# Small inputs in four host-laid arrays through SP's and ACT's queues, and 26 shared slots instead of 24, in a two-layer decoder trunk

## The chip, the cores and the metric

The kernel runs on one core of a Trainium2 chip. The metric is the time of one execution in microseconds on the device; lower is better. Five engines take part: TensorE (PE) for the matmuls, VectorE (DVE), ScalarE (ACT) and GpSimd (POOL) for work on vectors, and SyncE (SP), which here only issues DMAs. Each engine runs its own instructions in order, and semaphores tie the engines together. A DMA is issued by one engine and then runs on the 16 DMA engines that all of them share. PE's clock is granted by a throttle; the profile gives it as a share of full speed.

## The reference

```python
for l in range(DEPTH):                                   # 2 layers, 256 tokens, width 1024
    mix = token_mixer(x, w_in[l], ..., w_gate[l], b_gate[l], w_a[l], w_b[l], w_c[l], w_o[l], ...)
    x = layer_norm(alpha * x + mix, ln1_g[l], ln1_b[l])
    ffn = hier_moe(x, w_group[l], b_group[l], w_sub[l], b_sub[l], w1[l], w3[l], w2[l])
    x = layer_norm(alpha * x + ffn, ln2_g[l], ln2_b[l])

def hier_moe(...):
    g_prob = softmax(t @ w_group + b_group)              # 4 groups of experts, the best one is taken
    sub    = t @ w_sub + b_sub                           # 32 experts, the best two of that group
    ...
    for e in range(N_EXPERTS):                           # each a SwiGLU of width 256
        h = silu(t @ w1[e]) * (t @ w3[e])
        y = y + combine[:, e:e + 1] * (h @ w2[e])
```

The token mixer has three attention branches (latent, dilated, and sparse with a learned index) on one input projection; each branch is projected, multiplied by a gate and summed, and an output projection follows. All is float32. The inputs that the change concerns are the small ones: norm gains and biases (`q_norm_g`, `kv_norm_g`, `ln1_*`, `ln2_*`), gate biases and the router's weights and biases (`w_group`, `b_group`, `w_sub`, `b_sub`).

## The kernel before

Each of the two layers is a mixer and then an expert stage (`moe`). In the profile layer 0's mixer takes the first 290 us or so, its expert stage ends near 500; layer 1 is the same half again. The mixer's large matmuls are split in high and low parts (the lines 283 to 285), which makes them long; the expert stage goes through 32 experts in eight groups of four (`Q = 4`). For a group all four `w1` are used, then all four `w3` (both at L1697), then all four `w2` (L1777). An expert has three weights of 1 MiB: a group has 12 MiB.

All weights come through one pool of `NSLOT` shared slots, each 2048 floats (8 KB) in each of the 128 partitions, that is 1 MiB. The same slots hold other large tiles: `x`, the router's weights for the next layer (`wr`), the masks, and the gain rows (`gb`). The weights have a fixed order, the ring's queue. `Ring.pump` runs each time a slot is given back in the program and issues further weights as long as the plan (recorded in a dry run) says that slots suffice until their end (`fits`). So the ring runs ahead of the matmuls: where the program is about to work on one group, the issues of the next group or more already stand in SP's instruction stream. All weights are issued by SP, each with a wait for its slot's last reader. Eight DMA semaphores take turns for SP's transfers, and each issue waits for the transfer eight places ahead. In the last group of a layer `w3` comes in 16 transfers of 256 KB (four tiles, each with two of the eight parts of the width for all four experts), and `w2` in pieces of 512 KB and 256 KB; L195 issues whole tiles and L193 the pieces. The warm-up matmuls L291 work on no data of the result.

The small inputs are loaded by POOL. `load_small` (L398 to L417) fills `vec` row by row from seven arrays and the router's tile from two in a strided pattern, and the biases; for layer 0 at the start, for layer 1 in the expert stage of layer 0, after the third group (`e == 2 * Q`). `small_T` transposes `vec` on PE (L423) and scales the router on POOL; `small_rows` (L440) makes sums of it on PE. At L1326, in the mixer's output projection, `gpk` gets the first norm's gains in a packed form for the expert stage (L1660). At L1804, after the sixth group (`e == NE - 3 * Q`), `load_gains` (L447) takes a slot `gb` and loads the second norm's gain and bias as one row each; after the seventh group (`e == NE - 2 * Q`) `spread_gains` copies them to all partitions by eight PE passes (L458), and the last group follows.

The rules of the ring and the places of the gain row:

```python
while self.plan and not self.hold and self.queue and self.fits(self.queue[0][0]):
    self.issue()
...
if e == NE - 3 * Q:
    self.gb2 = self.load_gains(l, 2, 1)
...
if e == NE - 2 * Q:
    self.spread_gains(self.gb2)
```

Of the kernel before, what the change touches and what calls it, by code (L numbers as in the profile page):

```python
# [10 lines left out]
F32 = mybir.dt.float32  # L11
# [4 lines left out]
ALU = mybir.AluOpType  # L16
# [3 lines left out]
P = 128  # L20
L = 2
T = 256
NT = 2
D = 1024
KD = 8
# [19 lines left out]

WO = [(0, 512), (512, 256), (768, 256)]

NSLOT = 24
T1 = 5


# [61 lines left out]
CONSTS, MASKS = constants()  # L113
# [115 lines left out]
class Trunk:  # L229
# [26 lines left out]

    def tap(self, name, ap):
        if name in self.dbg:
            self.nc.gpsimd.dma_start(self.dbg[name], ap)
# [137 lines left out]

    def load_small(self, l, home, o):  # L398

        nc, a = self.nc, self.a  # L400
        v = self.v = self.t([P, P], F32, "vec", 1)
        nc.gpsimd.memset(v, 0.0)
        nc.gpsimd.dma_start(v[0:2], a["q_norm_g"][l].rearrange("(k p) -> k p", p=P))
        nc.gpsimd.dma_start(v[2:3], a["kv_norm_g"][l:l + 1])
        nc.gpsimd.dma_start(v[3:27], a["b_gate"][l].rearrange("(k p) -> k p", p=P))
        nc.gpsimd.dma_start(v[27:35], a["ln1_g"][l].rearrange("(k p) -> k p", p=P))
        nc.gpsimd.dma_start(v[35:43], a["ln1_b"][l].rearrange("(k p) -> k p", p=P))
        m = max(l - 1, 0)
        nc.gpsimd.dma_start(v[43:51], a["ln2_g"][m].rearrange("(k p) -> k p", p=P))
        nc.gpsimd.dma_start(v[51:59], a["ln2_b"][m].rearrange("(k p) -> k p", p=P))  # L410
        self.wgs = home
        self.wgb = home[:, o:o + KD * 72].rearrange("p (k f) -> p k f", k=KD)
        nc.gpsimd.dma_start(self.wgb[:, :, 36:40], a["w_group"][l].rearrange("(k p) f -> p k f", p=P))
        nc.gpsimd.dma_start(self.wgb[:, :, 40:72], a["w_sub"][l].rearrange("(k p) f -> p k f", p=P))
        self.br = self.t([1, 36], F32, "br", 1)
        nc.gpsimd.dma_start(self.br[:, 0:4], a["b_group"][l:l + 1])
        nc.gpsimd.dma_start(self.br[:, 4:36], a["b_sub"][l:l + 1])  # L417

    def small_T(self):

        nc = self.nc
# [7 lines left out]
        w = self.wgb[:, :, 36:72]  # L429
        for j in range(2):  # L430
            g = self.vec[:, 27 + 8 * j:35 + 8 * j, None].broadcast_to([P, KD, 36])
            nc.gpsimd.tensor_tensor(self.wgb[:, :, 36 * j:36 * j + 36], w, g, op=ALU.mult)
        nc.gpsimd.tensor_copy(self.wg, self.wgb[:, :, 0:36])

    def small_rows(self):

        nc = self.nc
        ps = self.bank()
        for k in range(KD):
            nc.tensor.matmul(ps[:, 0:72], self.one.broadcast_to([P, P]), self.wgb[:, k], start=k == 0, stop=False)  # L440
        nc.tensor.matmul(ps[:, 36:72], self.one[0:1].broadcast_to([1, P]), self.br, start=False, stop=True)
        self.wrow = self.t([P, 72], F32, "wrow", 1)
        nc.vector.tensor_copy(self.wrow, ps[:, 0:72])
        self.slots.free(self.wgs)

    def load_gains(self, l, which, rows=P):
        gb = self.slots.alloc([P, 2, D], F32, "gb")  # L447
        for j, n in enumerate(("g", "b")):
            self.nc.gpsimd.dma_start(gb[:rows, j], self.a[f"ln{which}_{n}"][l:l + 1].broadcast_to([rows, D]))
        return gb  # L450

    def spread_gains(self, gb):
# [846 lines left out]
    def mixer(self, l, acts):  # L1299
        nc = self.nc  # L1300
        prep, do = self.prep, self.do
        ps, nfill, n_wo = self.marks
        for a in START[l].split():
            if a in acts:
                acts[a]()
            elif a[0] == "m":
                do(int(a[1]), int(a[2]))
            else:
                self.lo_pool = a[0] == "P"
                prep(int(a[1:]))  # L1310
                self.lo_pool = False
        debt = 0.0
        for i in range(4, nfill - 4):
            need = ps[i][3]
            if need is not None and need not in self.seen:
                self.run_fg_until(need)
            for part in range(2):
                do(i, part)
                if part:
                    for j in range(1, 1 + (LA if i < LATE else LA_LATE)):  # L1320
                        prep(i + j)
                debt = self.run_fg(self.rate(i + 0.5 * part) / 2 + debt)
# [356 lines left out]
    def moe(self, l):  # L1679
        nc = self.nc  # L1680
# [8 lines left out]
        for e in range(0, NE, Q):  # L1689
# [238 lines left out]
def kernel(ctx: ExitStack, tc: tile.TileContext, a, out, dbg=None):  # L1928
# [3 lines left out]
    Trunk(tc, ctx, a, out, dbg, (dry.slots.log, dry.ring.ends)).run()  # L1932


_INS = ["x", "w_in", "q_norm_g", "w_uq", "kv_norm_g", "w_ukv", "w_gate", "b_gate", "w_a", "w_b", "w_c", "w_o",
        "ln1_g", "ln1_b", "w_group", "b_group", "w_sub", "b_sub", "w1", "w3", "w2", "ln2_g", "ln2_b"]


# [17 lines left out]
```

## Time and profile before

| | us |
|---|---|
| median of 3 runs | 1011.29 (1007.78 to 1011.47) |
| the profiled execution | 1009.72 |
| its span | 1008.0 |
| its clock granted to PE, mean | 0.953 of full speed |
| PE busy | 903.2 |
| DMA moved | 284.76 MB, 283 GB/s in the mean |

The profile is of one execution. Its page has the span in 40 slices (25.2 us each), the chain of work that ended last, the waits by line, and the DMA issues. The trace behind it gives a time line of each engine: the start of an instruction (or of a run of like ones), its length, and in brackets how long the engine had been idle and what ended that. The time line of SP shows when a DMA is issued; the table of DMAs says how long after that its data landed, as a median of the group.

### The profile page before, as it was taken

What the parts mean: (1) busy time and instruction counts of PE and PEld (TensorE: products, weight loads), DVE (VectorE), ACT (ScalarE), POOL (GpSimd) and SP (SyncE); (2) the same over time, 40 slices, a digit from 0 to 9 for tenths busy, and PEclk for the clock granted to TensorE, in tenths of its full rate; (3) what the DMA queues carried; (4) which work ended last, traced back from release to release, by engine and by line L of the source; (5) the groups of instructions that cost most, each with busy time, mean ns of one, the idle gap of its engine ahead of it and who ended that gap; (6) DMA issues with size and microseconds to landing.
All of it is one profiled execution on the core that took longest, in us unless ns stands there. A gap on an engine that the chain in (4) does not pass through costs nothing.

```text
span 1008.0 us, 18682 instructions
## 1 busy us (share of the span) xinstructions
PE 903.2 (90%) x7590; PEld 707.6 (70%) x7591; DVE 476.8 (47%) x968; ACT 419.4 (42%) x911; POOL 161.3 (16%) x274
## 2 busy tenths in 40 slices
PE   8999999999999976759879999999999998876595
PEld 7888899999985543435469888998999764443252
DVE  5848676944643100111398586777446521101014
ACT  5545655644462410122345645666344532210131
POOL 4531110012100110000156071100211000000001
PEclk9999999999999978789989999999999999877798
DMA  9933171596979999999992233516959799999995
GB/s 330 329 114 125 53 241 43 181 351 221 354 264 405 416 400 419 418 417 383 366 382 81 73 125 105 190 55 222 339 217 366 276 403 417 420 419 416 419 367 175
DMA packets 100170, 284.76 MB, mean 283 GB/s; under 512 B 6324, under 2 KB 53808, under 8 KB 78576
## 3 DMA queue, kind: packets, MB, share of 16 engines
q1 hardware_dynamic: 99088, 283.12, 74.5%
q8 instruction: 62, 1.02, 0.4%
q0 software_dynamic: 992, 0.39, 0.2%
q14 instruction: 28, 0.23, 0.1%
HBM read 282.44 MB, written 1.05 MB: 281 GB/s over the span
## 4 chain that ended last, share of the span: by engine, by line
PE 60%; DMA 22%; issue 7%; POOL 3%; DVE 3%; ACT 2%; SPq 1%; POOLq 0%; DVEq 0%; ACTq 0%
DMA w<-in_w_dram 20%; PE bank L283 13%; PE bank L284 12%; PE bank L285 12%; PE bank L1697 6%; PE bank L837 3%; PE bank L1777 2%; PE bank L891 2%; PE bank L878 2%; PE bank L1656 2%; DMA w<-in_w_in_dram 1%; PE bank L840 1%; PE bank L1763 1%; ACT xp L1438 1%; PE bank L1465 1%
## 5 line engine op out<-in xcount | busy, mean ns | idle before, releaser
L279 DVE TENSOR_TENSOR ws<-w,ws 128x1024 fp32r<-128x1024 f32 (+2 forms) x154 | 184.6, 1207 | 133.1 <-ACT ws L278 124.2
L1697 PE MATMUL bank<-w,xg 128*32 128x256 f32 x2048 | 150.0, 428 | 68.3 <-DMA w<-in_w_dram 59.1
L1697 PEld LDWEIGHTS bank<-w,xg 128*32 128x32 f32 x2048 | 71.9, 122 | 148.1 <-DMA w<-in_w_dram 70.1
L278 ACT ACTIVATE ws<-w 128x1024 fp32r<-128x1024 f32 (+2 forms) x158 | 158.9, 1023 | 35.7 <-PE bank L285 15.9
L283 PE MATMUL bank<-ws,xTh 128*128 128x408 f32 (+3 forms) x320 | 116.0, 362 | 1.2 <-ACT xTh L278 1.2
L283 PE MATMUL bank<-xTh,ws 128*128 128x256 f32 x384 | 111.2, 290 | 0.0
L285 PE MATMUL bank<-ws,xTl 128*128 128x408 f32 (+3 forms) x320 | 110.0, 344 | 1.1 <-DVE xTl L279 1.1
L284 PE MATMUL bank<-ws,xTh 128*128 128x408 f32 (+3 forms) x320 | 109.7, 343 | 0.2 <-DVE ws L279 0.2
L284 PE MATMUL bank<-xTl,ws 128*128 128x256 f32 x384 | 108.6, 283 | 0.0
L285 PE MATMUL bank<-xTh,ws 128*128 128x256 f32 x384 | 108.5, 283 | 0.0
L1727 DVE SCALAR_TENSOR_TENSOR t<-t,cw,bank 128x256 f32<-128x256 f32 x16 | 10.8, 677 | 200.5 <-PE bank L1697 200.5
L1660 ACT ACTIVATE xg<-bank,gpk 128x128 f32<-128x128 f32 x128 | 50.9, 453 | 95.3 <-PE bank L1656 92.7
L283 PEld LDWEIGHTS bank<-xTh,ws 128*128 128x128 f32 x384 | 73.5, 191 | 1.8 <-issue 1.0
L284 PEld LDWEIGHTS bank<-xTl,ws 128*128 128x128 f32 x384 | 73.6, 192 | 0.2
L285 PEld LDWEIGHTS bank<-xTh,ws 128*128 128x128 f32 x384 | 73.5, 191 | 0.0
L1722 ACT ACTIVATE t<-bank 128x256 f32<-128x256 f32 x16 | 6.2, 384 | 147.3 <-PE bank L1697 147.3
L283 PEld LDWEIGHTS bank<-ws,xTh 128*128 128x128 f32 x320 | 60.8, 190 | 8.1 <-ACT xTh L278 1.8
L853 ACT ACTIVATE p<-bank,nb 128x128 f32<-128x128 f32 (+1 forms) x92 | 37.3, 420 | 69.8 <-DVE nb L845 65.0
L285 PEld LDWEIGHTS bank<-ws,xTl 128*128 128x128 f32 x320 | 60.7, 190 | 6.2 <-DVE xTl L279 2.0
L1656 PE MATMUL bank<-xg,xp 128*128 128x128 f32 x512 | 63.0, 276 | 2.0 <-ACT xg L1660 2.0
L1656 PEld LDWEIGHTS bank<-xg,xp 128*128 128x128 f32 x512 | 60.6, 192 | 5.9 <-issue 2.5
L284 PEld LDWEIGHTS bank<-ws,xTh 128*128 128x128 f32 x320 | 60.9, 190 | 3.6 <-DVE ws L279 0.5
(361 smaller groups left out, 1587.6 us busy)
## 6 DMA issues: line engine op xcount, KB each, us to landing
w<-in_w_dram SPq DMA_DIRECT2D x168, 1024.0 KB, 19.0
w<-in_w_gate_dram SPq DMA_DIRECT2D x24, 1024.0 KB, 5.4
w<-in_w_dram SPq DMA_DIRECT2D x80, 256.0 KB, 6.9
w<-in_w_in_dram SPq DMA_DIRECT2D x18, 1024.0 KB, 9.6
w<-in_w_in_dram SPq DMA_DIRECT2D x12, 816.0 KB, 12.5
w<-in_w_o_dram SPq DMA_DIRECT2D x8, 1024.0 KB, 8.8
w<-in_w_a_dram SPq DMA_DIRECT2D x4, 1024.0 KB, 5.9
w<-in_w_c_dram SPq DMA_DIRECT2D x4, 1024.0 KB, 5.1
```

Source lines behind the costliest of these rows:

```text
L278: self.nc.scalar.activation(hi, src, AF.Copy)
L279: (self.nc.gpsimd if self.lo_pool else self.nc.vector).tensor_tensor(lo, src, hi.bitcast(F32), op=ALU.subtract)
L283: m(out, sh, mh, start=start, stop=False)
L284: m(out, sh, ml, start=False, stop=False)
L285: m(out, sl, mh, start=False, stop=stop)
L837: nc.tensor.matmul(b[:, j * w:(j + 1) * w], q[:, blk * P:(blk + 1) * P], k[:, 0:w], start=j == 0, stop=False)
L853: nc.scalar.activation(p[:, j], v[:, j], AF.Exp, bias=nb[:, j:j + 1], scale=u["scale"], accum_out=sm[:, j:j + 1])
L878: nc.tensor.transpose(ps[:, n * P:(n + 1) * P], p[:, j * P:(j + 1) * P], self.ident)
L891: nc.tensor.matmul(ps[half * 64:(half + 1) * 64, pr * P:(pr + 1) * P], u["v"](u["heads"][pr], kb), u["pt"][:, u["pt0"] + pr * nkb + kb], s ...
L1656: nc.tensor.matmul(ps[:, i * P:(i + 1) * P], self.xn[:, t, k + i], pm[:, t, j:j + Q].rearrange("p e c -> p (e c)"), start=t == 0, stop=t = ...
L1660: nc.scalar.activation(xg[:, k + i], ps[:, i * P:(i + 1) * P], AF.Identity, bias=b, scale=g)
L1697: nc.tensor.matmul(hp[i * CAP:(i + 1) * CAP, c * 256:(c + 1) * 256], xg[:, k, i * CAP:(i + 1) * CAP], w[i], start=k == 0, stop=k == KD - 1 ...
```

## The change

The host lays the small inputs out in four arrays: `vecs` (128 rows of 164 floats for each layer: the rows of `vec`, and the router's biases behind row 0), `router` (128 x 288), `gpk` (128 x 16) and `ln2` (one row of 2 x 1024). POOL issues no DMA any more. ACT loads `vecs` and `router` of layer 0 at the start; SP loads those of layer 1, `gpk` and `ln2`, at the same places of the program as before. As POOL issues nothing, its descriptor memory goes down to 64 bytes, and with the room that leaves the slots go from 24 to 26. The router's tile has the scaled and the plain weights as two blocks instead of side by side, with the views changed to fit.

```diff
-NSLOT = 24
+NSLOT = 26
...
     def load_small(self, l, home, o):
...
         nc, a = self.nc, self.a
-        v = self.v = self.t([P, P], F32, "vec", 1)
-        nc.gpsimd.memset(v, 0.0)
-        nc.gpsimd.dma_start(v[0:2], a["q_norm_g"][l].rearrange("(k p) -> k p", p=P))
...
-        nc.gpsimd.dma_start(v[51:59], a["ln2_b"][m].rearrange("(k p) -> k p", p=P))
+        eng = nc.sync if l else nc.scalar
+        small = self.t([P, P + 36], F32, "vec", 1)
+        eng.dma_start(small, a["vecs"][l])
+        self.v, self.br = small[:, 0:P], small[0:1, P:P + 36]
         self.wgs = home
-        self.wgb = home[:, o:o + KD * 72].rearrange("p (k f) -> p k f", k=KD)
-        nc.gpsimd.dma_start(self.wgb[:, :, 36:40], a["w_group"][l].rearrange("(k p) f -> p k f", p=P))
-        nc.gpsimd.dma_start(self.wgb[:, :, 40:72], a["w_sub"][l].rearrange("(k p) f -> p k f", p=P))
-        self.br = self.t([1, 36], F32, "br", 1)
-        nc.gpsimd.dma_start(self.br[:, 0:4], a["b_group"][l:l + 1])
-        nc.gpsimd.dma_start(self.br[:, 4:36], a["b_sub"][l:l + 1])
+        self.wgb = home[:, o:o + 2 * KD * 36].rearrange("p (j k f) -> p j k f", j=2, k=KD)
+        eng.dma_start(home[:, o + KD * 36:o + 2 * KD * 36], a["router"][l])
...
-    def load_gains(self, l, which, rows=P):
+    def load_gains(self, l):
         gb = self.slots.alloc([P, 2, D], F32, "gb")
-        for j, n in enumerate(("g", "b")):
-            self.nc.gpsimd.dma_start(gb[:rows, j], self.a[f"ln{which}_{n}"][l:l + 1].broadcast_to([rows, D]))
+        self.nc.sync.dma_start(gb[:1], self.a["ln2"][l:l + 1])
         return gb
...
             if i == n_wo - 12:
                 self.gpk = self.t([P, 2 * KD], F32, "gpk", 1)
-                for j, n in enumerate(("ln1_g", "ln1_b")):
-                    nc.gpsimd.dma_start(self.gpk[:, j * KD:(j + 1) * KD], self.a[n][l].rearrange("(p k) -> p k", p=P))
+                nc.sync.dma_start(self.gpk, self.a["gpk"][l])
...
             if e == NE - 3 * Q:
-                self.gb2 = self.load_gains(l, 2, 1)
+                self.gb2 = self.load_gains(l)
...
-    nc = _bacc.Bacc("TRN2", target_bir_lowering=False, num_devices=1)
+    nc = _bacc.Bacc("TRN2", target_bir_lowering=False, num_devices=1, dynamic_dma_scratch_size=64)
```

Where the change moves instructions, the built programs show it. The number behind a name is that of the tile; a `_49` in a wait only marks a semaphore.

SP before, late in layer 0's expert stage, where the weights of the last group are issued (`128x512` are pieces of `w3`, `128x2x512` of `w2`):

```order
L193 DMA w_4644<-in_w_dram 128x512 [waits DMAHW0_49,PE_49]
L193 DMA w_4644<-in_w_dram 128x512 [waits DMAHW1_49]
L193 DMA w_4644<-in_w_dram 128x512 [waits DMAHW2_49]
L193 DMA w_4644<-in_w_dram 128x512 [waits DMAHW3_49]
L193 DMA w_4649<-in_w_dram 128x2x512 [waits DMAHW4_49,PE_49]
L193 DMA w_4649<-in_w_dram 128x2x512 [waits DMAHW5_49]
L193 DMA w_4652<-in_w_dram 128x2x512 [waits DMAHW6_49,PE_49]
L193 DMA w_4652<-in_w_dram 128x2x512 [waits DMAHW7_49]
```

SP after, at the same place:

```order
L193 DMA w_4585<-in_w_dram 128x512 [waits DMAHW5_49,PE_49]
L193 DMA w_4585<-in_w_dram 128x512 [waits DMAHW6_49]
L193 DMA w_4585<-in_w_dram 128x512 [waits DMAHW7_49]
L193 DMA w_4585<-in_w_dram 128x512 [waits DMAHW0_49]
L193 DMA w_4590<-in_w_dram 128x2x512 [waits DMAHW1_49,PE_49]
L193 DMA w_4590<-in_w_dram 128x2x512 [waits DMAHW2_49]
L439 DMA gb_4593<-in_ln_dram 1x2048 [waits DMAHW3_49,PE_49]
L193 DMA w_4628<-in_w_dram 128x2x512 [waits DMAHW4_49,PE_49]
```

The gain row (`gb`, L439) now stands between the first and the second tile of the last group's `w2`, behind all `w3` of that group.

POOL before, where it loaded the gain row; the two rows ahead of it are its work on the router (`wr`) and on a gathered tile (`xg`):

```order
L433 COPY wg_4415<-wr_3907 128x288
L1647 TENSOR_TENSOR xg_3152<-xg_3152,comb_3098 128x256 [waits DVE_49] x2
L449 DMA gb_4608<-in_ln_g_dram 1x16x64 [waits DMAHW3_49,DMAHW1_49,DMAHW5_49,DMAHW0_49,DMAHW6_49,DMASW0_49,PE_49]
L449 DMA gb_4608<-in_ln_b_dram 1x16x64 [waits DMASW1_49]
L279 TENSOR_TENSOR ws_4992<-w_4699,ws_4992 128x832 [waits DMAHW3_49,DMAHW6_49,DMAHW0_49,DMAHW7_49,PE_49,Activation_49]
```

On POOL these two DMAs stood in a row of their own with no weights ahead of them; after the change POOL has none.

PE after, between the seventh group's last `w2` matmuls and the last group's first `w1` matmuls:

```order
L1766 MATMUL bank_4747<-w_4449,t_489_4712 32x512
L448 MATMUL bank_4768<-gb_4593,one 128x512 [waits DMAHW3_49,Activation_49]
L448 MATMUL bank_4771<-gb_4593,one 128x512 [waits DVE_49]
L448 MATMUL bank_4774<-gb_4593,one 128x512 [waits DVE_49]
L448 MATMUL bank_4777<-gb_4593,one 128x512 [waits DVE_49]
L1686 MATMUL bank_4784<-w_4451,xg_3438 32x256 [waits DMAHW5_49,DVE_49]
```

PE's order is the same as before; the first of the gain matmuls (L458 before, L448 after) waits for a transfer of SP's queue (`DMAHW3`), where it waited for one of POOL's (`DMASW0`).

## Rows read from the trace of the kernel before

**Rows 1.** The page: span, and PE and DMA by slices (tenths busy, 40 slices).

```profile
span 1008.0 us, 18682 instructions
...
PE   8999999999999976759879999999999998876595
...
DMA  9933171596979999999992233516959799999995
```

**Rows 2.** The page: the chain that ended last, by line, in shares of the span.

```profile
DMA w<-in_w_dram 20%; PE bank L283 13%; PE bank L284 12%; PE bank L285 12%; PE bank L1697 6%; PE bank L837 3%; PE bank L1777 2%; PE bank L891 2%; PE bank L878 2%; PE bank L1656 2%; DMA w<-in_w_in_dram 1%; PE bank L840 1%; PE bank L1763 1%; ACT xp L1438 1%; PE bank L1465 1%
```

**Rows 3.** Waits by line: us in total, times, longest us.

```profile
PE bank L1697 <- DMA w<-in_w_dram: 59.1, 15, 9.1
...
POOL wr L413 <- PE bank L1777: 20.8, 1, 20.8
...
POOL gb L449 <- PE bank L1777: 15.0, 2, 7.5
```

**Rows 4.** Time line of PE, layer 0's end: start, us, line, [idle before <- releaser].

```profile
449.04 1.06 PE L1697 MATMUL bank<-w,xg 128*32 128x256 f32 x2 [8.78 <-DMA w<-in_w_dram]
451.54 5.30 PE L1697 MATMUL bank<-w,xg 128*32 128x256 f32 x58 [1.44 <-DMA w<-in_w_dram]
457.31 3.66 PE L1697 MATMUL bank<-w,xg 128*32 128x256 f32 x64 [0.47 <-ACT t L1722]
...
470.54 3.69 PE L458 MATMUL bank<-gb,one 1*128 1x512 f32 x8
474.17 5.35 PE L1697 MATMUL bank<-w,xg 128*32 128x256 f32 x64
```

**Rows 5.** Time line of PE, layer 1's end.

```profile
947.95 1.06 PE L1697 MATMUL bank<-w,xg 128*32 128x256 f32 x2 [9.14 <-DMA w<-in_w_dram]
...
969.17 3.69 PE L458 MATMUL bank<-gb,one 1*128 1x512 f32 x8
```

**Rows 6.** Stretches: length; busy of PE, PEld, DVE, ACT, POOL; PEclk, DMA share, GB/s.

```profile
298.00:300.00 2.00, 2.00 (x44) 1.23 (x40) 0.42 (x1) 1.97 (x5) 0.00 (x0) 1.00 0.05 8
352.00:362.00 10.00, 2.43 (x16) 0.78 (x18) 0.69 (x1) 0.49 (x1) 2.89 (x4) 0.70 1.01 371
362.00:450.00 88.00, 63.98 (x623) 37.50 (x615) 10.11 (x21) 15.79 (x40) 5.33 (x9) 0.85 1.01 418
798.00:800.50 2.50, 2.50 (x49) 1.55 (x52) 0.42 (x1) 2.21 (x6) 0.00 (x0) 1.00 0.24 36
...
449.00:453.00 4.00, 2.52 (x18) 0.95 (x22) 0.00 (x0) 0.00 (x0) 0.00 (x0) 0.50 1.02 422
```

**Rows 7.** Time line of POOL, 435 to 445 us.

```profile
440.24 0.55 POOL L449 DMA_DIRECT2D gb<-in_ln_g_dram  x1 [7.50 <-PE bank L1777]
```

**Rows 8.** DMA issues: engine, count, KB each, median us from issue to landing.

```profile
w<-in_w_dram SPq DMA_DIRECT2D x168, 1024.0 KB, 19.0
...
cst<-in_consts_dram SPq DMA_DIRECT2D x1, 64.0 KB, 2.0
...
gb<-in_ln_g_dram POOLq DMA_DIRECT2D x2, 4.0 KB, 5.3
```

**Rows 9.** Time line of SP: first `w2` piece of the last group, layers 0 and 1.

```profile
478.12 0.75 SPq L193 DMA_DIRECT2D w<-in_w_dram  x1
...
976.75 0.57 SPq L193 DMA_DIRECT2D w<-in_w_dram  x1
```

**Rows 10.** DMA issues at 478.1 to 479.5 and 976.7 to 977.9 us.

```profile
w<-in_w_dram SPq DMA_DIRECT2D x2, 512.0 KB, 7.3
...
w<-in_w_dram SPq DMA_DIRECT2D x2, 512.0 KB, 7.0
```

**Rows 11.** Time line of ACT at the start: its first work on data.

```profile
5.92 1.09 ACT L278 ACTIVATE xTh<-bank 128x512 fp32r<-128x512 f32 x2 [3.66 <-PE bank L519]
```

**Rows 12.** Time line of SP at the start: the rest of the constants.

```profile
5.23 3.71 SPq L322 DMA_DIRECT2D cst<-in_consts_dram  x1
```

**Rows 13.** PE's transposes of the vectors: ns min/median/max, first and last start us.

```profile
L423 PE MATMUL bank<-cst,vec x2: 272/286/300, 32.6 to 411.6; 128*128 128x128 f32 x2
```

More of the change, by code (lines that the diff above doesn't have):

```diff
@@ L258, in tap @@
         if name in self.dbg:
-            self.nc.gpsimd.dma_start(self.dbg[name], ap)
+            self.nc.sync.dma_start(self.dbg[name], ap)
     def note(self, eng, n, psum=False):
@@ L400, in load_small @@
         nc, a = self.nc, self.a
-        v = self.v = self.t([P, P], F32, "vec", 1)
-        nc.gpsimd.memset(v, 0.0)
-        nc.gpsimd.dma_start(v[0:2], a["q_norm_g"][l].rearrange("(k p) -> k p", p=P))
[L404 to L409, printed above, removed]
-        nc.gpsimd.dma_start(v[51:59], a["ln2_b"][m].rearrange("(k p) -> k p", p=P))
-        self.wgs = home
-        self.wgb = home[:, o:o + KD * 72].rearrange("p (k f) -> p k f", k=KD)
-        nc.gpsimd.dma_start(self.wgb[:, :, 36:40], a["w_group"][l].rearrange("(k p) f -> p k f", p=P))
-        nc.gpsimd.dma_start(self.wgb[:, :, 40:72], a["w_sub"][l].rearrange("(k p) f -> p k f", p=P))
-        self.br = self.t([1, 36], F32, "br", 1)
-        nc.gpsimd.dma_start(self.br[:, 0:4], a["b_group"][l:l + 1])
-        nc.gpsimd.dma_start(self.br[:, 4:36], a["b_sub"][l:l + 1])
+        eng = nc.sync if l else nc.scalar
+        small = self.t([P, P + 36], F32, "vec", 1)
+        eng.dma_start(small, a["vecs"][l])
+        self.v, self.br = small[:, 0:P], small[0:1, P:P + 36]
+        self.wgs = home
+        self.wgb = home[:, o:o + 2 * KD * 36].rearrange("p (j k f) -> p j k f", j=2, k=KD)
+        eng.dma_start(home[:, o + KD * 36:o + 2 * KD * 36], a["router"][l])
     def small_T(self):
@@ L428, in small_T @@
         self.wg = self.t([P, KD, 36], F32, "wg", 1)
-        w = self.wgb[:, :, 36:72]
+        w = self.wgb[:, 1]
         for j in range(2):
             g = self.vec[:, 27 + 8 * j:35 + 8 * j, None].broadcast_to([P, KD, 36])
-            nc.gpsimd.tensor_tensor(self.wgb[:, :, 36 * j:36 * j + 36], w, g, op=ALU.mult)
-        nc.gpsimd.tensor_copy(self.wg, self.wgb[:, :, 0:36])
+            nc.gpsimd.tensor_tensor(self.wgb[:, j], w, g, op=ALU.mult)
+        nc.gpsimd.tensor_copy(self.wg, self.wgb[:, 0])
     def small_rows(self):
@@ L439, in small_rows @@
         for k in range(KD):
-            nc.tensor.matmul(ps[:, 0:72], self.one.broadcast_to([P, P]), self.wgb[:, k], start=k == 0, stop=False)
+            nc.tensor.matmul(ps[:, 0:72], self.one.broadcast_to([P, P]), self.wgb[:, :, k], start=k == 0, stop=False)
         nc.tensor.matmul(ps[:, 36:72], self.one[0:1].broadcast_to([1, P]), self.br, start=False, stop=True)
@@ L1932, with laid_out @@
     Trunk(tc, ctx, a, out, dbg, (dry.slots.log, dry.ring.ends)).run()
-_INS = ["x", "w_in", "q_norm_g", "w_uq", "kv_norm_g", "w_ukv", "w_gate", "b_gate", "w_a", "w_b", "w_c", "w_o",
-        "ln1_g", "ln1_b", "w_group", "b_group", "w_sub", "b_sub", "w1", "w3", "w2", "ln2_g", "ln2_b"]
+_INS = ["x", "w_in", "w_uq", "w_ukv", "w_gate", "w_a", "w_b", "w_c", "w_o", "w1", "w3", "w2"]
+def laid_out(a):
+    vecs = np.zeros((L, P, P + 36), np.float32)
+    for l in range(L):
+        m = max(l - 1, 0)
+        rows = [a["q_norm_g"][l], a["kv_norm_g"][l], a["b_gate"][l], a["ln1_g"][l], a["ln1_b"][l], a["ln2_g"][m], a["ln2_b"][m]]
+        v = np.concatenate([r.reshape(-1, P) for r in rows])
+        vecs[l, :len(v), :P] = v
+        vecs[l, 0, P:P + 4], vecs[l, 0, P + 4:] = a["b_group"][l], a["b_sub"][l]
+    router = np.concatenate([a["w_group"], a["w_sub"]], 2).reshape(L, KD, P, 36).transpose(0, 2, 1, 3).reshape(L, P, KD * 36)
+    gpk = np.concatenate([a[n].reshape(L, P, KD) for n in ("ln1_g", "ln1_b")], 2)
+    return {"vecs": vecs, "router": router, "gpk": gpk, "ln2": np.stack([a["ln2_g"], a["ln2_b"]], 1)}
 def kernel(**inputs):
@@ L1941 @@
     from concourse.bass_utils import run_bass_kernel_spmd as _run
-    nc = _bacc.Bacc("TRN2", target_bir_lowering=False, num_devices=1)
+    nc = _bacc.Bacc("TRN2", target_bir_lowering=False, num_devices=1, dynamic_dma_scratch_size=64)
     arrays, args = {}, {}
     feed = {n: inputs[n] for n in _INS}
-    feed["consts"], feed["masks"] = CONSTS, MASKS
+    feed.update(laid_out({n: np.asarray(a) for n, a in inputs.items()}), consts=CONSTS, masks=MASKS)
     for name, v in feed.items():
```

## The prediction

> **What bounds the kernel now.** I read the slices first. TensorE (PE) is busy nine tenths of the span, and its share dips at two places, late in the first half and at the end; there the DMA row stands at 9 [rows 1]. So the bound changes with the stage: PE in the mixers, the weight stream in the second part of each expert stage. The chain says the same: its largest single piece is the weights of the experts, a fifth of the span [rows 2]. The waits put a size on it: PE's expert matmuls (L1697) waited 59.1 us for weights [rows 3]. The last of these waits matter most, since what is late there ends late. In layer 0 PE stops at 449.04 for 8.78 us and at 451.54 for 1.44 us, and after that it stops for no DMA until the layer ends; the gain rows are spread at 470.54 (L458), and the first weights of the last group of four experts follow at 474.17 [rows 4]. Layer 1 repeats it about 499 us later: a wait of 9.14 us at 947.95, the gain rows at 969.17 [rows 5]. The stretch view tells since when the stream is saturated: between 298 and 300 the DMA engines are all but idle (8 GB/s), from 362 to 450 they move 418 GB/s; in layer 1 the idle stretch is 798 to 800.5 [rows 6]. Two consecutive tiles of 1 MiB let PE go on at 449.04 and 451.54: 2.50 us a tile [rows 4].
>
> **The change part by part.**
>
> **Two more slots.** The printed order shows each weight tile issued on the release that let the tile two places earlier go. At 298 to 300 the queue was empty for want of a slot; with two more slots two tiles more are then under way or done, and as the stream has no gap afterwards, each later landing comes two tiles sooner: 2 x 2.50 = 5.0 us. PE's last waits, 8.78 + 1.44 in layer 0 and 9.14 in layer 1, are longer than that, so PE passes them 5.0 us sooner in each layer, and so reaches the gain rows sooner. Bounds: 0 (if a release that is nearer to the end takes over) to 5.0; I take 5.0. By the Trainium skill ("DMA: Bandwidth & Descriptors", Specifications) memory gives a core about 358 GB/s; two tiles would then be 2.097 MB / 358 = 5.9 us. The trace does not agree: 418 GB/s over 88 us [rows 6].
>
> **POOL's router load goes.** In layer 0 POOL issues the next layer's router weights in scattered pieces at 352. From 352 to 362 the engines move 371 GB/s instead of 418 [rows 6]: 10 x (1 - 371/418) = 1.1 us are lost, and the 144 KiB that it carried are another 0.35. In their place 128 x 164 and 128 x 288 floats come in whole rows, 231 KB, 0.55 us at 418 GB/s. Net -0.9 in layer 0 (0 to -1.5), ahead of the last waits, so it counts: PE would come to the gain rows 5.9 us sooner, at 464.6, and in layer 1 5.0 sooner, at 964.2. SP must wait for the router's slot now, where POOL waited 20.8 us [rows 3]; what SP has in flight covers 19 us [rows 8], so at worst a gap of 2 us would follow. I take 0: SP comes to the slot later than POOL did, behind the tiles that the ring has run ahead with.
>
> **The gain row changes queues.** This decides. Before, POOL issues it from its own queue at 440.24 after a wait for a slot [rows 3, 7], it lands some 5.3 us later [rows 8], at about 446, and PE asks for it at 470.54: 24 us in hand. After, it stands in SP's queue, and SP is not where PE is. The order of SP shows it behind the four w1 tiles of the last group, its 16 quarter-megabyte pieces of w3 and the first two pieces of its w2, all of which the ring has queued by running ahead. Yet PE needs it *before* any of the last group's weights. A SP transfer is issued only when the one eight places ahead of it has landed (the order prints that wait on every row), and those in flight are served in turn: a 1 MiB tile lands 19 us after its issue [rows 8]. So the row's landing is that of its neighbours. The two w2 pieces ahead of it were issued before at 478.12 and 0.8 us later [rows 9] and landed 7.3 us after issue in the median [rows 10]: in the mean at 478.5 + 7.3 = 485.8; half a megabyte takes 1.3 us at 400 GB/s, so the second lands at 486.4. In layer 1: 976.75 and 0.6 later [rows 9], median 7.0 [rows 10], so 977.1 + 7.0 + 0.65 = 984.7. Taking off the stream's lead, and 0.1 for the 8 KB themselves:
> layer 0: 486.4 - 5.9 + 0.1 = 480.6, where the gain rows were spread at 470.54: +10.1 us;
> layer 1: 984.7 - 5.0 + 0.1 = 979.8, where it was 969.17: +10.6 us.
> PE would stand still for 480.6 - 464.6 = 16 us, and 15.6. All the lead is spent, and more. What comes next, the last group and the norm, is fed by weights that have landed by then or land soon after, so it follows unchanged; a queue that SP fills a few tiles ahead cannot become late by PE's pause.
> Bounds: no earlier than the issue allows. Its issue follows the second w2 piece's by 0.7 us, at 479.6 - 5.9 = 473.7 (when the eleventh w3 piece, eight places ahead, has landed); the shortest landing in the trace is 2.0 us (the 64 KB constants at the start, with an empty queue [rows 8]): 475.7, still +5.2 in layer 0 and about +5 in layer 1. The upper bound is 1 us more than I took. I take the neighbours' landing since SP's other transfers landed one after the other.
> The rows speak for separate queues: POOL's row landed in 5.3 us while SP's tiles took 19 [rows 8]. By the Trainium skill ("DMA: Bandwidth & Descriptors", Issuing engines are not separate DMA queues) the engine that issues a transfer saves only its own sequencer's time, since all run on the same 16 engines and interleave. By that rule alone the row would land as POOL's did, 5.3 us after its issue, at 479.0, and the sum would be 3 us smaller for both layers. The trace agrees with the shared engines, but shows a transfer of the other queue served well ahead of older ones.
>
> **The clock after the pause.** After the 8.78 us wait PE's granted clock is 0.50 from 449 to 453 (the lower of its two levels, 1.2 instead of 2.4 GHz) [rows 6], and 58 matmuls take 5.30 us where 64 take 3.66 at full clock [rows 4]: 5.30 - 58/64 x 3.66 = 2.0 us. The new pause is longer, and what follows it (eight gain matmuls, 3.69 us at full clock, then 64 of L1697) runs into the same: +2.0 us a layer. Bounds 0 (L1697 at 474.17 already ran at 5.35 instead of 3.66, so the loss may only change places) to 4.
>
> **The start.** ACT now issues two transfers ahead of its table load, the second after the first has landed: 0.4 + 2.0 [rows 8] + 0.4 = 2.8 us. It sat idle 3.66 us before its first work on data at 5.92 [rows 11], which hides it. The 231 KB share the engines with the first inputs: +0.6, bounded by 0 below and by 2.5 above: SP's issue of its constants took 3.71 us [rows 12], and if the router's took as long ACT would be ready at 0.8 + 0.4 + 2.0 + 3.7 + 1.5 = 8.4 instead of 5.92.
>
> **No cost.** The packed gains and layer 1's vectors and router also stand in SP's queue now, but with room. The vectors are loaded three groups ahead of the gain row, and a group has 12 MiB of weights, 30 us at 2.50: they land about 480.6 - 90 = 391 (an estimate), where PE transposes them at 411.6 [rows 13], or 405.7 with the lead; those 15 us cover them, and without that cover each late microsecond would cost one. The packed gains are asked for ahead of the last part of the mixer, where the stream still has idle stretches [rows 1, 6]. POOL's issues and its memset go; nothing waits for them now. The tap is not used.
>
> **Sum.** Span 1008.0 [rows 1] + 0.6 + (10.1 + 2.0) + (10.6 + 2.0) = 1033.3; 1.7 us lie outside the span in the profiled execution (1009.72), so 1035.0. The median shown is 1011.29, 1.6 above that execution; half of that on top, near 1036. I say **1035.5**, some 2.4% slower.
>
> **Rivals.**
> *The row overtakes the stream* (slower by less). For it: its one row needs few of the 16 engines, and one that is ahead of the others may be done early. Against it: each engine has its share of the pieces ahead. At the lower bound, 475.7, PE loses 5.2 + 5 us, with the clock term between 0 and 2 a layer: 1009.7 + 0.6 + 10.2 + 0 to 4 = 1020 to 1025.
> *The lead wins* (faster). If the row were at hand when PE asks, at 464.6 and 964.2, nothing is left but 1008.0 + 0.6 - 5.9 - 5.0 = 997.7 in the span, 999.4, or 1000 against the median. That needs the stream to be some 16 us, over six tiles, further ahead than before at that place, or the row to be issued in front of the last group. The point from which it decides is the row's landing at 470.5 (969.2): later is slower, earlier is faster. Two slots are two tiles, and the printed order has the row behind the group; little speaks for it.
> *Nothing comes of either* (no change). If the two slots bring no lead, there is no gain to set against the stall; if the row lands about at 470, the two cancel: 1006 to 1016. This takes both a landing before the lower bound and a start that costs nothing.
> *The slots aren't used* (the change doesn't do what it says): the stream keeps its pace, the row lands at 486.5 - 0.9 and 984.8, so 15.1 and 15.6 us late, and with the clock and the start it is 1009.7 + 30.7 + 4 + 0.6 = 1045. The order speaks against it.
>
> **How the numbers follow.** Stalls in both layers at the neighbours' landing, with the bounds of clock and start (1027 to 1041): 0.70. Overtaking: 0.14. Slots unused or a clock that stays low: 0.05. The lead wins: 0.06. Cancelling: 0.05. A measurement of this kernel tells 0.5%, about 5 us, from no change. The range 1018 to 1041 holds the first two, 0.8 and a little more. Faster 0.06, within 0.5% 0.05, slower 0.89.
>
> **What would show it.** In the profile after: PE's wait at the gain matmuls (L448 there), about 16 us in each layer, released by a DMA of SP's queue that lands at 480 to 481 of layer 0's clock, the longest wait of the kernel; the two waits of 8.78 and 1.44 shrunk by 5 to 6 us together; no DMA idle near 298; 418 GB/s through 352 to 362; a clock of about 0.5 in the 4 us after the pause; POOL's queue all but empty. Wrong if the wait at the gain matmuls is under 5 us, or if it is long and the layer's end isn't later by two thirds of the wait.

## The result and the profile after

The changed kernel takes 1033.22 us in the median (1032.88 to 1034.14) where the kernel before took 1011.13: a ratio of 1.0227, 95% interval 1.0207 to 1.0246. It is slower by 2.3%, and the forecast was 1035.5 in a range of 1018 to 1041.

The page of the changed kernel: the span, PE and DMA in 40 slices, and the chain by line. They answer to [rows 1] and [rows 2].

```profile
span 1031.4 us, 18616 instructions
...
PE   8999999999999867774879999999999999566765
...
DMA  9933351795889999999952144436968899999961
...
DMA w<-in_w_dram 29%; PE bank L283 12%; PE bank L284 12%; PE bank L285 12%; PE bank L1686 3%; PE bank L827 3%; DMA w<-in_w_in_dram 2%; PE bank L881 2%; SPq L195 2%; PE bank L868 2%; DMA gb<-in_ln_dram 1%; PE bank L1766 1%; PE bank L830 1%; ACT xp L1427 1%; PE bank L1645 1%
```

PE's dips at the two layer ends are deeper than before, and the weights' part of the chain has grown from a fifth to 29%, with the gain row (`gb`) in the chain, where it did not stand before. The waits of PE by line, with total, times and longest in us, name it:

```profile
PE bank L1686 <- DMA w<-in_w_dram: 51.9, 15, 8.8
PE bank L448 <- DMA gb<-in_ln_dram: 28.0, 2, 14.2
```

The first row answers to the 59.1 us of [rows 3]; the second is new, once a layer. PE's time line at the end of layer 0, with start, length and in brackets the idle time before and what ended it, answers to [rows 4]:

```profile
441.90 1.06 PE L1686 MATMUL bank<-w,xg 128*32 128x256 f32 x2 [8.75 <-DMA w<-in_w_dram]
444.38 5.48 PE L1686 MATMUL bank<-w,xg 128*32 128x256 f32 x58 [1.42 <-DMA w<-in_w_dram]
...
477.87 7.16 PE L448 MATMUL bank<-gb,one 1*128 1x512 f32 x8 [14.23 <-DMA gb<-in_ln_dram]
484.97 5.68 PE L1686 MATMUL bank<-w,xg 128*32 128x256 f32 x64
```

PE passes its last wait for weights at 441.90 instead of 449.04, stands ready for the gain row at 477.87 - 14.23 = 463.6, and waits until 477.87; the eight gain matmuls then take 7.16 us instead of 3.69. The last two waits for weights are as long as before (8.75 and 1.42 us against 8.78 and 1.44): they begin and end sooner. The lead shows at the first waits of layer 0's expert stage. The kernel before had two of 4.63 and 2.94 us, the changed kernel has two of 1.57 and 0.22; the first of each, before and after:

```profile
356.80 1.06 PE L1697 MATMUL bank<-w,xg 128*32 128x256 f32 x2 [4.63 <-DMA w<-in_w_dram]
...
352.77 3.64 PE L1686 MATMUL bank<-w,xg 128*32 128x256 f32 x58 [1.57 <-DMA w<-in_w_dram]
```

The chain in order of time, over the same stretch, says what the row itself waited for:

```profile
446.88 18.01 DMA w<-in_w_dram
...
464.96 5.14 DMA w<-in_w_dram
...
470.87 0.60 SPq L193
...
471.57 6.17 DMA gb<-in_ln_dram
```

A weight that is issued at 446.88 lands at 464.89; its landing lets the transfer eight places behind it go at 464.96; that one's landing at 470.11 lets SP issue two `w2` pieces and then, in its turn, the row at 471.57. Before, POOL issued the row at 440.24 [rows 7]. Layer 1 does the same (first weight wait, gain matmuls, next weights):

```profile
953.07 1.06 PE L1686 MATMUL bank<-w,xg 128*32 128x256 f32 x2 [8.30 <-DMA w<-in_w_dram]
...
989.03 7.16 PE L448 MATMUL bank<-gb,one 1*128 1x512 f32 x8 [13.81 <-DMA gb<-in_ln_dram]
996.12 6.10 PE L1686 MATMUL bank<-w,xg 128*32 128x256 f32 x64
```

Three stretches (length; busy of PE, PEld, DVE, ACT, POOL; granted clock, DMA share, GB/s) and ACT's first instructions complete the picture:

```profile
296.00:298.00 2.00, 1.92 (x29) 1.10 (x31) 0.42 (x1) 1.98 (x7) 0.42 (x1) 1.00 0.03 12
...
352.00:362.00 10.00, 8.54 (x125) 4.63 (x126) 0.77 (x3) 0.38 (x1) 0.00 (x0) 1.00 1.01 420
...
480.00:484.00 4.00, 4.00 (x6) 1.38 (x5) 1.28 (x2) 0.60 (x1) 0.00 (x0) 0.50 1.10 349
```

```profile
0.76 0.40 ACTq L404 DMA_DIRECT2D vec<-in_vecs_dram  x1
3.09 0.38 ACTq L408 DMA_DIRECT2D masks<-in_router_dram  x1
3.50 1.28 ACT L1345 ACT_TABLE_LOAD   x1 [3.37 <-DMA vec<-in_vecs_dram]
...
5.83 1.09 ACT L278 ACTIVATE xTh<-bank 128x512 fp32r<-128x512 f32 x2 [0.83 <-PE bank L509]
```

From 352 to 362 the stream moves 420 GB/s now, where it was 371 [rows 6]: POOL's scattered load is gone. The stretch near 298 in which the DMA engines idle is still there, a little sooner (12 GB/s from 296 to 298). The clock after the pause is 0.50, the lower level. At the start ACT's wait between its two transfers fits into the idle time that it had: its first work on data begins at 5.83 instead of 5.92 [rows 11].

### The profile page after: what moved, and what is told of

Read it like the earlier page. It is cut to its first block, busy times and chain, and to the rows that moved or that the text cites. A ratio compares the mean times of both kernels' runs of the same rounds, so it can differ in the third digit from the quotient of the medians.

```text
span 1031.4 us, 18616 instructions
## 1 busy us (share of the span) xinstructions
PE 905.8 (88%) x7584; PEld 708.0 (69%) x7591; DVE 478.0 (46%) x968; ACT 419.4 (41%) x911; POOL 144.5 (14%) x242
## 4 chain that ended last, share of the span: by engine, by line
PE 54%; DMA 32%; issue 5%; POOL 2%; SPq 2%; DVE 2%; ACT 2%; POOLq 0%; DVEq 0%
DMA w<-in_w_dram 29%; PE bank L283 12%; PE bank L284 12%; PE bank L285 12%; PE bank L1686 3%; PE bank L827 3%; DMA w<-in_w_in_dram 2%; PE bank L881 2%; SPq L195 2%; PE bank L868 2%; DMA gb<-in_ln_dram 1%; PE bank L1766 1%; PE bank L830 1%; ACT xp L1427 1%; PE bank L1645 1%
## 5 line engine op out<-in xcount | busy, mean ns | idle before, releaser
L1686 PE MATMUL bank<-w,xg 128*32 128x256 f32 x2048 | 148.0, 423 | 61.1 <-DMA w<-in_w_dram 51.9
L1686 PEld LDWEIGHTS bank<-w,xg 128*32 128x32 f32 x2048 | 71.1, 121 | 141.3 <-DMA w<-in_w_dram 62.2
L1645 PE MATMUL bank<-xg,xp 128*128 128x128 f32 x512 | 63.0, 276 | 2.0 <-ACT xg L1649 2.0
L1645 PEld LDWEIGHTS bank<-xg,xp 128*128 128x128 f32 x512 | 60.6, 192 | 5.9 <-issue 2.5
```

Source lines behind the costliest of these rows:

```text
L1645: nc.tensor.matmul(ps[:, i * P:(i + 1) * P], self.xn[:, t, k + i], pm[:, t, j:j + Q].rearrange("p e c -> p (e c)"), start=t == 0, stop=t = ...
L1686: nc.tensor.matmul(hp[i * CAP:(i + 1) * CAP, c * 256:(c + 1) * 256], xg[:, k, i * CAP:(i + 1) * CAP], w[i], start=k == 0, stop=k == KD - 1 ...
```

## Experiments

Theory: the small row stands behind weights that the ring has queued ahead, and that alone costs 2.3%; the two slots are worth about 5 us a layer as soon as the row is out of the way. Rivals: PE would have stood still there anyway for other data; the transfer as such is slow; the loss comes from another of the moved loads.

**The row moved forward in SP's own queue.** One line of the changed kernel:

```diff
-            if e == NE - 3 * Q:
+            if e == NE - 4 * Q:
                 self.gb2 = self.load_gains(l)
```

> The changed kernel, the gain row still in SP's queue, but loaded one group of four experts earlier in the program. Theory: it then stands about 30 us of stream further ahead, lands near 450 in layer 0, and PE doesn't wait for it: 997 to 1001, plus up to 2.5 us a layer since the row holds one of the slots for one group longer: 997 to 1006. Rival (the transfer as such, one row of 8 KB into one partition, is what is slow on SP's queue): a wait at the gain matmuls remains, 1010 or more.

Measured: 1000.47 us (999.89 to 1002.67), ratio to the kernel before 0.9907 (0.9887 to 0.9927). PE no longer waits for the row, and the lead stays; the end of layer 0 on PE's time line:

```profile
442.04 1.06 PE L1686 MATMUL bank<-w,xg 128*32 128x256 f32 x2 [8.24 <-DMA w<-in_w_dram]
444.52 5.96 PE L1686 MATMUL bank<-w,xg 128*32 128x256 f32 x58 [1.42 <-DMA w<-in_w_dram]
...
464.18 5.12 PE L448 MATMUL bank<-gb,one 1*128 1x512 f32 x8
```

SP issues the row at 434.62 and PE uses it at 464.18. So the 33 us between this version and the changed kernel hang on the row's place in the queue, not on the transfer. The slot that the row holds for a group longer shows no cost with 26 slots: the last weight wait ends at 442.04, against 441.90. This version is faster than both kernels, than the kernel before by 0.9%.

**Only the row moved, in the kernel before.**

```diff
-            self.nc.gpsimd.dma_start(gb[:rows, j], ...)
+            self.nc.sync.dma_start(gb[:rows, j], ...)
```

> The kernel before with one thing changed: the two gain rows are issued by SP instead of POOL; 24 slots, all other small loads on POOL. Theory (this part alone does the harm): the rows land with the third w3 tile, 480 in layer 0 and 978 in layer 1, 9 to 10 us after PE used to begin there; with 3 to 4 us of low clock a layer, less half a microsecond where the tail waited for w2: 1033 to 1037. Rival (the stall needs the deeper run-ahead of 26 slots, or comes from another of the moved loads): 1009 to 1013.

Measured: 1031.36 us (1030.82 to 1032.20), 1.0210 (1.0193 to 1.0227). The change of queue alone, with 24 slots and all else left, does as much harm as the whole change. It is 1.6 us below the expected range; the row had landed by 477.80 instead of 480. PE's wait is 7.32 us in layer 0:

```profile
477.93 7.16 PE L458 MATMUL bank<-gb,one 1*128 1x512 f32 x8 [7.32 <-DMA gb<-in_ln_g_dram]
```

**The changed kernel with 24 slots.**

```diff
-NSLOT = 26
+NSLOT = 24
```

> The changed kernel with 24 slots instead of 26. By its order the gain row then stands behind three of the four w3 tiles of the last group and ahead of w2 (with 26 slots: behind all four and the first w2 tile). Theory: the stream loses its lead of two tiles, but the row stands two tiles nearer to the front, so it lands at 479 to 480 of layer 0, nearly as with 26 slots, and PE waits for about 9 to 10 us instead of 14: 1032 to 1036, the two slots being worth next to nothing while the row stands in SP's queue. Rival (the slots carry their 5 us a layer whatever the row does): 1043.

Measured: 1028.31 us (1028.12 to 1029.01), 1.0179 (1.0162 to 1.0196): below the range that was expected, and 5 us faster than with 26 slots. With the row in SP's queue two more slots do harm. PE's last weight wait and the gain matmuls in layer 0, and the end of the row's chain:

```profile
447.33 1.06 PE L1686 MATMUL bank<-w,xg 128*32 128x256 f32 x2 [9.31 <-DMA w<-in_w_dram]
...
476.15 7.16 PE L448 MATMUL bank<-gb,one 1*128 1x512 f32 x8 [7.56 <-DMA gb<-in_ln_dram]
```

```profile
462.26 10.67 DMA w<-in_w_dram
...
472.99 3.02 DMA gb<-in_ln_dram
```

Between 24 and 26 slots PE's last weight wait in layer 0 moves from 447.33 to 441.90: the lead of two tiles is 5.4 us. But the ring also queues two tiles more ahead of the row, 18 pieces of the last group instead of 12. SP's time line with 24 and with 26 slots:

```profile
452.35 20.27 SPq L193 DMA_DIRECT2D w<-in_w_dram  x12
...
446.88 24.59 SPq L193 DMA_DIRECT2D w<-in_w_dram  x18
```

The first piece is issued 5.5 us sooner, but the row follows it after 24.7 us instead of 20.6, so the row is issued only 1.4 us sooner, at 471.57 instead of 472.99. And it takes 6.17 us to land behind 512 KB pieces, 3.02 behind pieces of 256 KB. So PE begins the gain matmuls at 477.87 instead of 476.15. The 3.02 us were not expected: the 256 KB piece that SP issued just ahead of it, 0.7 us sooner, took 5.2 by the table of DMAs (count, KB, us from issue to landing):

```profile
w<-in_w_dram SPq DMA_DIRECT2D x1, 256.0 KB, 5.2
```

So the row overtook pieces that were ahead of it. In the trace it is a single packet of 8 KB that takes 0.3 us; it starts 2.4 us after its issue with 24 slots and 5.4 us after it with 26. The transfer as such is not slow, then: the row waits, first of all for its issue and then for its turn.

**The two slots with the row out of the way.** The version with the row one group earlier, with 24 slots.

> The changed kernel with the gain row loaded one group earlier (as in the version that ran at 1000.5) and 24 slots instead of 26. Theory: with the row out of the way the two slots are worth two tiles a layer, 5.0 us or a little more (5.4 measured at layer 0's last weight wait between the changed kernel with 24 and with 26 slots), so this version takes 1010 to 1012. Rival (the earlier row alone carries the gain, slots are worth nothing): 1000 to 1003.

Measured: 1008.36 us (1005.40 to 1012.05), 0.9988 (0.9968 to 1.0009), a little under the range that was expected and no different from the kernel before, against 0.9907 with 26 slots. The slots are worth some 8 us then (0.0081 x 1011). At the weight waits they bring more than at the end. Layer 0 and layer 1, each with the last weight wait, the gain matmuls and the next weights; ahead of them the first matmul of layer 1, by which layer 1's times are to be counted (495.10 in the version with 26 slots):

```profile
449.42 1.06 PE L1686 MATMUL bank<-w,xg 128*32 128x256 f32 x2 [8.81 <-DMA w<-in_w_dram]
...
470.98 3.70 PE L448 MATMUL bank<-gb,one 1*128 1x512 f32 x8
...
500.29 1.39 PE L1502 MATMUL bank<-cst,x 128*128 128x128 f32 x8 [0.52 <-DVE x L1490]
```

```profile
946.84 1.06 PE L1686 MATMUL bank<-w,xg 128*32 128x256 f32 x2 [8.29 <-DMA w<-in_w_dram]
...
968.86 3.70 PE L448 MATMUL bank<-gb,one 1*128 1x512 f32 x8
972.48 3.66 PE L1686 MATMUL bank<-w,xg 128*32 128x256 f32 x64
```

and layer 1 of the version with 26 slots:

```profile
936.12 1.06 PE L1686 MATMUL bank<-w,xg 128*32 128x256 f32 x2 [7.52 <-DMA w<-in_w_dram]
...
958.69 4.70 PE L448 MATMUL bank<-gb,one 1*128 1x512 f32 x8
963.32 5.98 PE L1686 MATMUL bank<-w,xg 128*32 128x256 f32 x64
```

At layer 0's last wait the two slots are worth 449.42 - 442.04 = 7.4 us (of that 2.1 come with the row's earlier place, 449.42 against 447.33 with 24 slots; in layer 1 no such cost shows, 446.55 against 446.86 from that layer's first matmul), at layer 1's 446.55 - 441.02 = 5.5. By layer 0's end 5.2 us of the 7.4 are left (500.29 against 495.10), by the end of layer 1 1.9 of the 5.5, counted from there (1005.7 - 500.29 against 998.6 - 495.10, by the spans). In layer 1 PE gives 0.6 us back in the 58 matmuls behind the wait (6.37 against 5.81), 1.0 in the gain matmuls (4.70 against 3.70) and 2.3 in the next weights (5.98 against 3.66). The last two ran at full clock without the lead (3.70 and 3.66 us) and at a low one with it, in the mean 0.69 of full speed from 958 to 969:

```profile
958.00:969.00 11.00, 11.00 (x80) 4.23 (x72) 2.41 (x4) 1.79 (x3) 0.00 (x0) 0.69 0.99 352
```

**The row on ACT's queue instead of SP's.**

```diff
-        self.nc.sync.dma_start(gb[:1], self.a["ln2"][l:l + 1])
+        self.nc.scalar.dma_start(gb[:1], self.a["ln2"][l:l + 1])
```

> The changed kernel with one line different: the gain row is issued by ACT instead of SP, at the same place of the program; 26 slots and all else as changed. Theory (the row is late only because it stands behind the weights in SP's queue): it lands within about 6 us of its issue, before PE asks; the wait of about 14 us at the gain matmuls is gone in both layers, and the rest of the lead shows: 997 to 1001 us. Rival 1 (PE would have waited there anyway, for the last group's weights): 1020 or more, with the wait at L1686 instead of L448. Rival 2 (any hardware-queue transfer is served behind the weights in flight, whoever issues it): row lands some 15 to 20 us after its issue, still before PE, so the same time as the theory, but seen in the landing.

Measured: 1045.93 us (1044.21 to 1049.23), 1.0354 (1.0326 to 1.0383). None of the three expectations fits: the time is over 1020 with the wait at L1686, as rival 1 had it, but PE waits for ACT there and not for weights, and already in the seventh group. ACT's time line and PE's:

```profile
437.66 0.60 ACT L278 ACTIVATE y<-bank 128x512 fp32r<-128x512 f32 x1 [1.20 <-PE bank L1766]
474.79 0.52 ACTq L439 DMA_DIRECT2D gb<-in_ln_dram  x1
475.36 0.38 ACT L1711 ACTIVATE t<-bank 128x256 f32<-128x256 f32 x1 [37.10 <-DMA w<-in_w_dram]
```

```profile
475.79 6.22 PE L1686 MATMUL bank<-w,xg 128*32 128x256 f32 x64 [21.17 <-ACT t L1711]
```

ACT could not issue the row before 474.79, and its next activation, for which PE waited 21.17 us, stood behind. The built program says why: SP's and ACT's transfers share eight semaphores, handed out in turn in the order of the program. ACT's row got the semaphore of a `w3` piece that SP had been given ahead of it, and it may be issued only when that piece has landed. So the run-ahead holds a transfer of ACT's as it holds one of SP's, and on ACT work stands behind it. In the kernel before, POOL's transfers go by semaphores of their own (`DMASW0` and `DMASW1` in the printed order). Once issued, the row was not held up: on ACT's queue its packet of 8 KB starts at 478.67 and takes 0.3 us, so it is through some 4 us after its issue, with weights in flight that took 7 to 8. On this the theory was right and rival 2 wrong.

**The same, one group earlier,** to test that explanation: the row on ACT's queue and loaded at `e == NE - 4 * Q`.

> The gain row issued by ACT, and one group earlier in the program. Theory on why ACT's issue at the old place made it 1046 us (a transfer on a hardware queue takes the next of eight semaphores that SP's and ACT's transfers share in program order, and waits for the landing of the one that had it before; behind the run-ahead that is a weight landing some 20 us later, and ACT's own work stands behind the wait): ACT is held just the same, one group earlier, by the landing of a weight at about 434 while it gets there near 411; 1015 to 1045 us, a wait of 15 to 25 us of PE on ACT in the group. Rival (only the last group's 256 KB pieces, or the end of the layer, held it): no such wait, 998 to 1003.

Measured: 1008.47 us (1006.26 to 1012.91), 0.9986 (0.9970 to 1.0003). ACT was held as expected, from about 405 until 434.88, and PE waited 14.70 us for it in layer 0 (16.90 in layer 1):

```profile
434.88 0.49 ACTq L439 DMA_DIRECT2D gb<-in_ln_dram  x1
435.47 0.38 ACT L1711 ACTIVATE t<-bank 128x256 f32<-128x256 f32 x1 [30.53 <-DMA gb<-in_ln_dram]
```

```profile
435.91 6.08 PE L1686 MATMUL bank<-w,xg 128*32 128x256 f32 x64 [14.70 <-ACT t L1711]
451.44 3.64 PE L1686 MATMUL bank<-w,xg 128*32 128x256 f32 x64
```

But the time is below the 1015 to 1045 that were expected. The stream goes on while PE stands still, and the seventh group's weights are all there at 451.44, where the other versions wait 8 us for them. A pause ahead of the last weight wait is paid for largely out of that wait; the same pause one group later, in the run above, finds none to be paid from. So of the theory the mechanism held and the price did not.

**The clock's part of the loss.** In the changed kernel, 60 warm-up matmuls into PE's pause:

```diff
             if e == NE - 2 * Q:
+                self.warm(60, self.mk)
                 self.spread_gains(self.gb2)
```

> The changed kernel with 60 warm-up matmuls of no use (some 13 us at full clock) put ahead of the gain matmuls, into the 14 us in which PE waits for the row; the result is the same. Theory (the pause costs a second time through the clock, as the gain matmuls then take 7.16 us instead of 3.69): the gain matmuls take 3.7 us, the time falls by 6 to 8 us, to 1025 to 1027. Rival 1 (the slow clock belongs to the one-partition gain matmuls themselves): they stay at 7 us, 1032 to 1034. Rival 2 (the saved time is given back, since the last group's weights land too late): gain matmuls 3.7 us, but a wait at the last group's weights, over 1030.

Measured: 1028.17 us (1027.00 to 1030.69), 1.0186 (1.0164 to 1.0209): 4 to 5 us less than the changed kernel (5.1 by the medians, 4.1 by the two ratios to the kernel before), short of the 6 to 8 expected. Layer 0 and layer 1:

```profile
463.81 13.12 PE L291 MATMUL bank<-mk 128*128 128x512 bf16 x60
478.40 3.67 PE L448 MATMUL bank<-gb,one 1*128 1x512 f32 x8 [1.47 <-DMA gb<-in_ln_dram]
...
985.65 5.44 PE L448 MATMUL bank<-gb,one 1*128 1x512 f32 x8 [1.08 <-DMA gb<-in_ln_dram]
```

In layer 0 the gain matmuls are back at 3.67 us, so the 7.16 do not belong to the one-partition matmuls themselves (rival 1); in layer 1 they are at 5.44 only: there the clock was low for a part in spite of the warm-up. So the second price of the pause, a low clock after it, is shown, at 4 to 5 of the 22 us.

**Warm-up ahead of the last weight wait,** in the version with the row one group earlier (32 matmuls ahead of the seventh group's first weights).

> The version with the row loaded one group earlier, 26 slots, and 32 warm-up matmuls ahead of the seventh group's first weights, in the 8 us in which PE waits for them. Theory: the clock is full when the weights come, the 58 matmuls behind the wait take about 3.5 us instead of 5.7 to 6.4 and the gain matmuls 3.7 instead of 4.7 to 5.1; 3 to 4 us a layer, 993 to 996 us. Rival (the end of the layer is set by the landing of the last weights, so that the lead turns into a wait there): 998 to 1001.

Measured: 997.57 us (995.16 to 1000.88), 0.9868 (0.9848 to 0.9887). The matmuls behind the wait took 5.33 and 6.50 us, against 5.96 and 6.37 without it, so the expected 3.5 us did not show there. In layer 0 the gain matmuls and the 64 behind them did run at full clock (3.69 and 3.66 us, against 5.12 and 5.57 without it). The two versions were run again together:

> The version with the gain row one group earlier and 26 slots, once more, beside the one with warm-up matmuls on the same chip: 999 to 1002 us.

> The same with 32 warm-up matmuls ahead of the seventh group's first weights, once more. Its first profile showed the matmuls behind the last weight wait as slow as without the warm-up (5.3 and 6.5 us), against what was expected, while its median was lower by 3 us on another chip. Theory (the warm-up doesn't help, since the clock is low again when the weights come): within 1 us of the version without it. Rival (it helps somewhere else): 2 us or more below it.

Measured: 998.93 us (995.15 to 1003.46), 0.9885 (0.9858 to 0.9912) without the warm-up, 997.63 (995.93 to 1000.65), 0.9879 (0.9861 to 0.9898) with it. The difference is 1.3 us, within the intervals: whether the warm-up gives any time is not settled. In this second profile with it the mechanism does show in layer 0. Layer 0 and layer 1, the matmuls behind the wait:

```profile
446.36 3.64 PE L1688 MATMUL bank<-w,xg 128*32 128x256 f32 x58 [1.87 <-DMA w<-in_w_dram]
...
939.12 5.22 PE L1688 MATMUL bank<-w,xg 128*32 128x256 f32 x58 [1.87 <-DMA w<-in_w_dram]
```

The version without the warm-up took 6.11 and 6.34 us for them. So the same warm-up kept the clock up behind the wait in one of the four places, and why not in the others stays open.

## Why the prediction was right

- **What decides:** right. The row's place in SP's queue costs 33 us against the same transfer one group earlier, and the change of queue alone makes the kernel before 2.1% slower.
- **The two slots:** 5.0 us a layer; measured between the changed kernel with 24 and with 26 slots 5.4 in layer 0, and in layer 1, counted from that layer's first matmul (508.91 and 510.87), 955.77 - 508.91 against 953.07 - 510.87, so 4.7. Right at the weight waits. The lead came as forecast: by 298 us the changed kernel had moved 225 GB/s in the mean, the kernel before 218, which is 2.1 MB or two tiles more. Two of the signs that were named for it did not come: the idle stretch near 298 is still there, now behind two more tiles, and the last two waits did not shrink, as PE comes to them sooner by the lead. The prediction did not say that the slots also queue more in front of the row, and that they thus add to the loss.
- **The router load of POOL:** undersized. With 24 slots the last weight wait ended at 447.33 against 449.04 before, so all of the change but the slots brought 1.7 us by there, where -0.9 was taken and -1.5 was the bound. How much of that is the router load was not tried.
- **The row's landing:** 480.6 was forecast, 477.74 came (PE began at 477.87). Of the 2.9 us, 2.1 are the issue, at 471.57 instead of 473.7: 1.2 of them the larger lead (7.1 us at PE's last wait instead of 5.9), most of the rest that the 16 pieces of `w3` were issued in 23.3 us instead of 24.0. The other 0.7 are the way from issue to landing, 6.17 us instead of 6.9. In layer 1, which began 10.35 us later (510.87 against 500.52), the gain matmuls came 989.03 - 10.35 - 969.17 = 9.5 us later instead of 10.6. The argument that the row lands with its neighbours gave nearly the right time here, but it is not the rule: with 24 slots it overtook some of them. The bound rested on the issue, which waits for the transfer eight places ahead; that mechanism was right, but the row was issued 2.1 us before the time that was given as the earliest.
- **The rule on issuing engines:** by it the row would have landed 5.3 us after its issue, as POOL's did. By the Trainium skill ("DMA: Bandwidth & Descriptors", Issuing engines are not separate DMA queues) the DMAs of all issuing engines run on the same 16 DMA engines and interleave, whichever engine started them. The row took 6.17 us in the changed kernel, where it landed within 0.2 us of the piece ahead of it, and 3.02 us with 24 slots, sooner than by either reckoning; a row of 4 KB on SP's queue in the kernel before took 2.79. So neither gives the time. What both leave open, when the transfer can be issued at all, made the difference here.
- **The clock:** undersized. 2.0 us a layer were taken; the gain matmuls took 3.47 us longer and the 64 matmuls behind them 0.33 in layer 0 and 0.75 in layer 1, so 3.8 and 4.2, at the upper bound of 4. Some 0.7 us a layer came back at the end. In layer 0 nearly all of it lies in the last `w2` matmuls: at full clock 16 of them took 1.24 and 1.55 us before and take 1.07 now, so they no longer seem to wait for weights that came in late. In layer 1 0.25 us of it lies there.
- **The start:** +0.6; PE's second batch of input transposes began at 9.33 against 8.85, so +0.5 there; ACT's wait was hidden as forecast. It did not last: the first expert stage's L1645 (L1656 before) has its 24 matmuls begin at 291.26 against 292.24.
- **No cost:** right. SP issued layer 1's vectors at 367.63 and the router at 370.16, and PE's waits for their work, 2.2 and 1.8 us, are those of the kernel before.
- **The sum:** 12.1 and 12.6 us a layer with 0.6 at the start made 25.3; it came to 10.35 (the start within it) and 13.05, so 23.4. The landings were 3.8 us too late in the forecast and the clock's price 4.0 us too small; the two errors offset each other, and what came back at the layers' ends makes up most of the rest. That they offset each other is luck. So the total is better than its terms.

Of the rivals, the lead that wins came true as soon as the row was moved: 1000 was worked out, 1000.47 and 998.93 were measured. That the lead shrinks towards the layers' ends there, as matmuls run at a low clock, was not in that rival's sum; the 1.1 us more at layer 0's last wait (7.0 instead of 5.9) made up for some of it. Why the clock is lower there with the lead than without was not tried.

## What to carry to other kernels

A queue that runs ahead turns program order into arrival order: a small load that is asked for soon belongs ahead of what the prefetch has queued, so look at where its issue stands among the prefetches, not at its size. A deeper prefetch makes this worse while it helps the stream: here two slots more cost 5 us with the row behind the prefetch and gave some 8 with the row ahead of it. And where the pause falls decides its price: ahead of the last wait for the stream it is paid largely out of that wait, behind it in full, and then once more in the clock.

## What the runs showed of the hardware that was not expected

- A transfer issued by ACT waited for a weight of SP's queue to land, since the two engines' transfers share the eight semaphores of this program in turn: ACT was held from 437.66 + 0.60 until 474.79.
- A row of 8 KB landed 3.02 us after its issue while a 256 KB piece issued 0.7 us ahead of it took 5.2: in one queue a small transfer can land ahead of larger ones. Behind pieces of 512 KB it took 6.17. The row is one packet, which itself took 0.3 us.
- 13 us of warm-up matmuls that ended 1.1 us before the row came kept the gain matmuls at full clock in layer 1 for a part only (5.44 us against 3.67). The same 32 warm-up matmuls ahead of a wait for weights left 58 matmuls at 5.33 us in one run and at 3.64 in the next.
